# A two-layer hybrid backbone on one core: the splits of queries and keys keep the place in which they are traced

## The chip, the cores and the metric

The kernel runs on 1 core of one Trainium2 chip. The metric is the time of one execution on the device in microseconds (us); the median of 3 runs is given, and one execution was profiled. The engines are named as the profile names them: PE (TensorE, with PEld for its weight loads), DVE (VectorE), ACT (ScalarE), POOL (GpSimd), SP (the engine that issues most DMAs).

## The reference, cut to what matters

The model has two layers over 512 latent tokens and 256 context tokens of width 1024. Each layer is a half-step SwiGLU FFN, four parallel groups of heads over one input projection, an output projection, and a second half-step FFN. The change touches two of the four groups, both attention:

```
for l in range(DEPTH):                        # 2
    need_ctx = l < DEPTH - 1                  # the last layer gives no context output
    ...
    ya = s5_mixer(...)                        # a state-space scan
    yb = natten_mixer(q, k, v, rpb)           # neighbourhood attention, 4 heads of 64, bias table
    yc = gqa_mixer(q, k, v, gq, gk)           # 4 query heads, 2 key heads, qk-RMSNorm, rotary
    yd = rglru_mixer(...)                     # a gated recurrence
    h = h + gate * (concatenate([ya, yb, yc, yd]) @ w_out)

s = einsum('bqhgd,bkhd->bhgqk', q, k); p = softmax(s); o = einsum('bhgqk,bkhd->bqhgd', p, v)
```

Latent queries read context and latent keys (768 in all), context queries only context keys. In neighbourhood attention a latent query reads a window of 8 rows by 16 columns, plus the context. All of it is float32.

## The kernel before

**Precision by splitting.** PE multiplies in a float32 format of fewer bits (fp32r). A float32 operand x is therefore split into hi, its rounding to fp32r, and lo = x - hi. For the scores of attention the query tile holds hi of a head in 64 of its 128 partitions and lo in the other 64 (`stack_q`), and the key tiles hold kh (the hi part, once in each half) and kl (the lo part, once in each half). Two matmuls then give the score: one with kl as its moving operand (L796), one with kh (L797).

**The steps.** A split is an ACT instruction (the cast to hi: L963, L974, L984), then a DVE instruction that reads it (the subtraction: L964, L975, L985). Keys must then be copied to the other 64 partitions, which takes DMAs that POOL issues: in `stack_k` (gqa) one L977 for hi and one for lo, in `stack_ks` (neighbourhood attention, na) two L988 each for hi and lo, which fill the tiles of the second head from rows 64 to 128, and then one L989 each, which overwrites rows 64 to 128 of the first head's tile with its rows 0 to 64. So an L989 has to follow the two L988 that read what it overwrites. All of these copies are of 64 x 768 floats, 192 KB.

**The order of attention.** `attention()` (L817) goes through four groups: gqa(0), gqa(1), na(0), na(1). A group has 12 units in layer 0 (8 of latent queries and 4 of context queries) and 8 in layer 1. A unit has three stages: scores and softmax; transposes of the probabilities (L813, copied out by L815); the product with the values (L865). The stages of a unit stand 0, 2 and 3 units apart (LAGS), so that PE goes from one unit's scores to the transposes of another. The softmax is one DVE instruction (L805: add the bias or scale, take the maximum) and one of ACT (L806: exp). Each group has preparing steps, which are traced a few units ahead of its first unit: in gqa keys two units ahead and queries one, in na the bias 4, the keys 3, the queries 2 and the values 1 unit ahead. na also builds bias tiles on POOL (L1047 clears one, L1048 adds table and mask). In the last units of na(1) `part` splits finished rows for the output projection on POOL, L693 for hi and L696 for lo. Where an input projection is finished, `evac` takes it out of PSUM on DVE (L675, L679, L681).

**What sets the order.** The Tile framework traces the program and a scheduler (schedule_with_timeline_sim=True) orders each engine's instructions, by its own simulated timeline. `keep_in_program_order`, held as `self.pin`, makes an instruction keep its traced place among the pinned ones. In this kernel only PE's instructions in attention are pinned: scores (L796, L797), transposes (L813) and products with the values (L865). Each engine works through its order without skipping.

Of the kernel before, what the change touches and what calls it, by code (L numbers as in the profile page):

```python
# [10 lines left out]
F32 = mybir.dt.float32  # L11
F32R = mybir.dt.float32r
AF = mybir.ActivationFunctionType
ALU = mybir.AluOpType
# [6 lines left out]
TT = TL + TC  # L21
# [577 lines left out]
class Mixer:  # L599
# [357 lines left out]
    def stack_q(self, src, nt, scale=1.0, tag="g"):  # L957

        nc, out = self.nc, []
        for hh in range(2):  # L960
            a, b = 64 * hh, 64 - 64 * hh
            q = self.n.t(tag, F32R)
            nc.scalar.activation(q[a:a + 64, :nt], src[a:a + 64, :nt], AF.Copy, scale=scale)  # L963
            nc.vector.scalar_tensor_tensor(q[b:b + 64, :nt], src[a:a + 64, :nt], scale, q[a:a + 64, :nt].bitcast(F32),  # L964
                                           ALU.mult, ALU.subtract)
            out.append(q)
        return out

    def stack_k(self, src, hh, tag="g"):

        nc = self.nc
        a, b = 64 * hh, 64 - 64 * hh
        kh, kl = self.n.t(tag, F32R), self.n.t(tag, F32R)
        nc.scalar.copy(kh[a:a + 64, :TT], src[a:a + 64, :])  # L974
        nc.vector.tensor_sub(kl[a:a + 64, :TT], src[a:a + 64, :], kh[a:a + 64, :TT].bitcast(F32))  # L975
        for k in (kh, kl):
            nc.gpsimd.dma_start(k[b:b + 64, :TT], k[a:a + 64, :TT])  # L977
        return kh, kl

    def stack_ks(self, src):  # L980

        nc = self.nc
        kh, kl, kh2, kl2 = (self.n.t("g", F32R) for _ in range(4))
        nc.scalar.copy(kh[:, :TT], src)  # L984
        nc.vector.tensor_sub(kl[:, :TT], src, kh[:, :TT].bitcast(F32))  # L985
        for k, k2 in ((kh, kh2), (kl, kl2)):
            for a in (0, 64):
                nc.gpsimd.dma_start(k2[a:a + 64, :TT], k[64:128, :TT])  # L988
            nc.gpsimd.dma_start(k[64:128, :TT], k[0:64, :TT])  # L989
        return (kh, kl), (kh2, kl2)  # L990
# [679 lines left out]
```

## Time and profile before

| | us |
|---|---|
| median of 3 runs | 2868.43 (2867.08 to 2870.94) |
| profiled execution, time on the device | 2865.24 |
| its span | 2863.5 |
| busy in the span: PE | 2800.9 (98%) |
| DVE | 1730.1 (60%) |
| ACT | 909.4 (32%) |
| POOL | 759.4 (27%) |

The times of instructions below count from the start of the span. Attention lies at about 800 to 945 us in layer 0 and at 2305 to 2415 in layer 1; most of the rest is PE at work on the projections and the FFNs. In the rows a line number is that of the code, tiles are named without their running numbers, "x2" is two instructions in a row, and a bracket at the end of a row tells how long the engine sat idle before it and whose work ended that.

### The profile page before, as it was taken

The page shows a single profiled execution, that of the slowest core. Times are in us where ns is not written, and L with a number is a line of the kernel's source. Part 1 is how long each engine was busy: PE and PEld are TensorE (multiplying, and loading weights), DVE is VectorE, ACT ScalarE, POOL GpSimd, SP SyncE. Part 2 cuts the span into 40 slices and gives each one's busy share as a digit, 9 for nine tenths or more (in the row PEclk, how much of TensorE's full clock was granted, in tenths as well). Part 3 has the DMA queues.
Part 4 walks back from the last instruction along what each step waited for, and adds up shares of the span by engine and source line. Part 5 has one row for each costly group of instructions (what it writes and reads, how often), then busy time and mean ns, then how long its engine had stood idle before and what let it go on. Part 6 is the DMA issues. An engine that isn't in the chain of part 4 may idle for free.

```text
span 2863.5 us, 43435 instructions
## 1 busy us (share of the span) xinstructions
PE 2800.9 (98%) x17293; PEld 2429.0 (85%) x17293; DVE 1730.1 (60%) x3130; ACT 909.4 (32%) x1478; POOL 759.4 (27%) x957
## 2 busy tenths in 40 slices
PE   7999999999999999999999999999999999999998
PEld 4888888888877888888888888888888888899998
DVE  6868477676857566464634775465565876444445
ACT  3212122235546422212213321222224655322223
POOL 2822243222323311000001266423412434201001
PEclk8999999999999999999999999999999999999999
DMA  6445334354324333232212335233254444222231
GB/s 226 137 109 168 111 98 136 112 183 137 105 62 86 104 100 114 76 109 96 97 51 68 116 102 138 89 120 97 81 160 142 120 119 101 77 94 83 89 96 53
DMA packets 295900, 312.12 MB, mean 109 GB/s; under 512 B 58991, under 2 KB 243202, under 8 KB 295698
## 3 DMA queue, kind: packets, MB, share of 16 engines
q1 hardware_dynamic: 266990, 293.97, 32.2%
q0 software_dynamic: 5664, 12.59, 1.9%
q10 hardware_dynamic: 23044, 2.78, 0.7%
q8 instruction: 137, 2.24, 0.3%
q14 instruction: 65, 0.53, 0.1%
HBM read 276.09 MB, written 29.02 MB: 107 GB/s over the span
## 4 chain that ended last, share of the span: by engine, by line
PE 72%; DVE 5%; issue 1%; DMA 1%; ACT 1%; POOL 1%; SPq 0%; DVEq 0%; ACTq 0%; POOLq 0%
PE pi L390 41%; PE po L390 20%; PE po L1239 4%; PE po L865 1%; DVE acc L256 1%; PE pt L813 1%; PE ps L796 1%; PE pl L737 1%; DMA wa<-in_w_ada_dram 1%; DVE wl L380 1%; PE ps L797 0%; PE pa L263 0%; DMA W<-s5w 0%; PE px L1146 0%; DMA wr<-in_w_ffn_out_dram 0%
## 5 line engine op out<-in xcount | busy, mean ns | idle before, releaser
L390 PE MATMUL pi<-g,wh 128*128 128x258 f32 (+2 forms) x6656 | 1408.1, 330 | 8.2 <-DVE l L681 3.1
L390 PEld LDWEIGHTS pi<-g,wh 128*128 128x128 f32 x6656 | 1100.3, 191 | 131.8 <-issue 14.6
L390 PE MATMUL pi<-g,wl 128*128 128x258 f32 (+2 forms) x3328 | 825.3, 328 | 0.7 <-DVE wl L380 0.7
L379 ACT CAST wh<-wr 128x1024 fp32r<-128x1024 f32 (+3 forms) x380 | 339.0, 892 | 1405.2 <-PE pi L390 669.7
L390 PEld LDWEIGHTS pi<-g,wl 128*128 128x128 f32 x3328 | 607.0, 191 | 59.4 <-DVE wl L380 1.5
L390 PE MATMUL po<-l,wh 128*128 128x512 f32 (+1 forms) x2464 | 566.3, 344 | 1.2 <-DVE e L496 0.8
L390 PEld LDWEIGHTS po<-l,wh 128*128 128x128 f32 x2464 | 387.8, 188 | 64.3 <-issue 3.8
L460 POOL TENSOR_TENSOR l<-z,l 128x768 fp32r<-128x768 f32 (+1 forms) x88 | 159.0, 1806 | 1065.0 <-ACT l L459 958.9
L380 DVE TENSOR_TENSOR wl<-wr,wh 128x1024 fp32r<-128x1024 f32 (+3 forms) x380 | 404.3, 1064 | 54.3 <-ACT wh L379 51.5
L256 DVE SCALAR_TENSOR_TENSOR acc<-wa,s,acc 128x512 f32<-128x512 f32 x448 | 358.3, 849 | 40.8 <-DMA wa<-in_w_ada_dram 40.0
L496 DVE SCALAR_TENSOR_TENSOR e<-po,gt,e 128x512 f32<-128x512 f32 (+1 forms) x296 | 176.2, 631 | 305.2 <-PE po L390 251.2
L390 PE MATMUL po<-l,wl 128*128 128x512 f32 (+1 forms) x1232 | 337.1, 343 | 1.0 <-DVE wl L380 0.9
L454 DVE TENSOR_TENSOR z<-pi,R 128x768 f32<-128x768 f32 (+2 forms) x91 | 78.4, 865 | 301.3 <-PE pi L390 301.3
L390 PEld LDWEIGHTS po<-l,wl 128*128 128x128 f32 x1232 | 194.5, 188 | 32.9 <-DVE wl L380 2.4
L449 DVE COPY bc<-pi 128x2 f32<-128x2 f32 x88 | 13.8, 157 | 187.7 <-PE pi L390 187.7
L459 ACT CAST l<-z 128x768 fp32r<-128x768 f32 (+1 forms) x88 | 69.0, 784 | 160.9 <-DVE z L456 160.9
L1548 POOL TENSOR_TENSOR ww<-AR,BB 128x256 f32<-128x256 f32 x32 | 25.1, 786 | 338.2 <-PE pw L1567 306.8
L456 DVE SCALAR_TENSOR_TENSOR z<-z,pi,z 128x512 f32<-128x512 f32 (+1 forms) x154 | 107.8, 735 | 5.5 <-ACT z L452 0.8
L317 POOL TENSOR_TENSOR ssq<-ssq,sq 128x768 f32<-128x768 f32 (+1 forms) x35 | 67.8, 1936 | 161.6 <-ACT sq L316 161.6
L452 ACT ACTIVATE z<-z,bc 128x512 f32<-128x512 f32 (+1 forms) x154 | 90.3, 627 | 61.0 <-DVE z L450 49.9
L450 DVE TENSOR_TENSOR z<-pi,R 128x768 f32<-128x768 f32 (+1 forms) x88 | 77.5, 881 | 3.7 <-ACT R L367 3.7
L1239 PE MATMUL po<-l,wh 128*128 128x512 f32 (+1 forms) x264 | 72.0, 356 | 0.0
(349 smaller groups left out, 2597.9 us busy)
## 6 DMA issues: line engine op xcount, KB each, us to landing
wr<-in_w_ffn_in_dram SPq DMA_DIRECT2D x88, 1024.0 KB
wa<-in_w_ada_dram SPq DMA_DIRECT2D x64, 1024.0 KB
wr<-in_w_ffn_out_dram SPq DMA_DIRECT2D x48, 512.0 KB
wr<-in_w_ffn_out_dram SPq DMA_DIRECT2D x32, 640.0 KB
wr<-in_w_in_dram SPq DMA_DIRECT2D x16, 1024.0 KB
W<-s5w SPq DMA_DIRECT2D x32, 256.0 KB
wr<-in_w_out_dram SPq DMA_DIRECT2D x8, 1024.0 KB
l<-in_w_ada_dram SPq DMA_DIRECT2D x24, 256.0 KB
```

What stands on the lines that cost most here:

```text
L256: nc.vector.scalar_tensor_tensor(acc[r], raw[:, k], s, acc[r], ALU.mult, ALU.add)
L379: nc.scalar.copy(hi[:, :kn], raw[:, :, o:o + P])
L380: nc.vector.tensor_sub(lo[:, :kn], raw[:, :, o:o + P], hi[:, :kn].bitcast(F32))
L390: nc.tensor.matmul(dst, lhsT=wt[:, k, :], rhs=xt[:, a:b], start=(k == 0 and i == 0), stop=(k == kn - 1 and i == 2))
L450: nc.vector.tensor_mul(ta[:, :nt], pa[:, 256:256 + nt], self.R[:, :nt])
L452: nc.scalar.activation(ta[:, a:b], ta[:, a:b], AF.Silu, bias=bc[:, i:i + 1])
L454: nc.vector.tensor_mul(tb[:, a:b], p, self.R[:, a:b])
L456: nc.vector.scalar_tensor_tensor(tb[:, a:b], tb[:, a:b], pb[:, 254 + i:255 + i], ta[:, a:b], ALU.add, ALU.mult)
L459: nc.scalar.copy(uh[:, :nt], tb[:, :nt])
L460: nc.gpsimd.tensor_sub(ul[:, :nt], tb[:, :nt], uh[:, :nt].bitcast(F32))
L496: self.nc.vector.scalar_tensor_tensor(self.h[j][:, a:b], ps[:, a:b], gate[:, j, i:i + 1], self.h[j][:, a:b], ALU.mult, ALU.add)
L1239: self.nc.tensor.matmul(dst, lhsT=wt[:, k, :], rhs=xt[:, a:b], start=(c == 0 and i == 0), stop=(c == NT - 1 and i == 2))
```

## The change

The ACT and the DVE instruction of each split are given to `self.pin`: six instructions in three functions. Nothing else is edited.

```diff
@@ stack_q
-            nc.scalar.activation(q[a:a + 64, :nt], src[a:a + 64, :nt], AF.Copy, scale=scale)
-            nc.vector.scalar_tensor_tensor(q[b:b + 64, :nt], src[a:a + 64, :nt], scale, q[a:a + 64, :nt].bitcast(F32),
-                                           ALU.mult, ALU.subtract)
+            self.pin(nc.scalar.activation(q[a:a + 64, :nt], src[a:a + 64, :nt], AF.Copy, scale=scale))
+            self.pin(nc.vector.scalar_tensor_tensor(q[b:b + 64, :nt], src[a:a + 64, :nt], scale, q[a:a + 64, :nt].bitcast(F32),
+                                                    ALU.mult, ALU.subtract))
@@ stack_k
-        nc.scalar.copy(kh[a:a + 64, :TT], src[a:a + 64, :])
-        nc.vector.tensor_sub(kl[a:a + 64, :TT], src[a:a + 64, :], kh[a:a + 64, :TT].bitcast(F32))
+        self.pin(nc.scalar.copy(kh[a:a + 64, :TT], src[a:a + 64, :]))
+        self.pin(nc.vector.tensor_sub(kl[a:a + 64, :TT], src[a:a + 64, :], kh[a:a + 64, :TT].bitcast(F32)))
@@ stack_ks
-        nc.scalar.copy(kh[:, :TT], src)
-        nc.vector.tensor_sub(kl[:, :TT], src, kh[:, :TT].bitcast(F32))
+        self.pin(nc.scalar.copy(kh[:, :TT], src))
+        self.pin(nc.vector.tensor_sub(kl[:, :TT], src, kh[:, :TT].bitcast(F32)))
```

The built programs show what moves. A row gives the line, the operation, the tile written and the tiles read with their running numbers, and the shape; - is a row that stood here before, + one that stands here now.

VectorE in layer 0, in the first half of gqa(0). L975 of g_7993 is the lo of gqa(1)'s keys, the L964 of g_8033 and g_8036 of its queries, L985 of g_8304 and g_8637 the lo of the keys of na(0) and na(1), the L964 of g_8329 and g_8332 the queries of na(0):

```order
 L380 TENSOR_TENSOR wl_9081<-wr_9078,wh_9080 128x1024
-L975 TENSOR_TENSOR g_7993<-e_6807,g_7992 64x768
-L964 SCALAR_TENSOR_TENSOR g_8033<-e_6682,g_8033 64x768
-L964 SCALAR_TENSOR_TENSOR g_8036<-e_6682,g_8036 64x768
-L985 TENSOR_TENSOR g_8304<-l_7567,g_8303 128x768
-L964 SCALAR_TENSOR_TENSOR g_8329<-l_7407,g_8329 64x768
-L964 SCALAR_TENSOR_TENSOR g_8332<-l_7407,g_8332 64x768
-L985 TENSOR_TENSOR g_8637<-l_7665,g_8636 128x768
 L675 COPY bc_7971<-pi_7922 128x2
```

All seven leave this place and stand further down in the order, spread over the units of gqa(0), gqa(1) and na(0); the evacuation (L675) now follows the weight split (L380) at once.

POOL in layer 0, in the last units of na(0), ahead of na(1). g_8636 and g_8637 are kh and kl of the first head of na(1), g_8638 and g_8639 those of the second; e_8739 and e_8740 are bias tiles of na(1), l_8934 and l_8952 hi parts for the output projection:

```order
+L988 DMA g_8638<-g_8636 64x768 x2
+L988 DMA g_8639<-g_8637 64x768 x2
 L1047 MEMSET e_8739 128x256
 L1048 TENSOR_TENSOR e_8739<-e_8596,e_8257 128x256
 L1047 MEMSET e_8740 128x256
+L989 DMA g_8636<-g_8636 64x768
 L1048 TENSOR_TENSOR e_8740<-e_8605,e_8257 128x256
 L693 TENSOR_SCALAR l_8934<-z_7427 128x768
 L693 TENSOR_SCALAR l_8952<-z_7430 128x768
+L989 DMA g_8637<-g_8637 64x768
```

The six copies for na(1) stood before na(0)'s bias tiles, right behind those for na(0); now they stand in the last units of na(0), and that of kl comes behind two L693.

POOL in layer 1, at the same place. g_21858 and g_21859 are kh and kl of the first head of na(1), g_21860 and g_21861 those of the second. Before:

```order
L977 DMA g_21301<-g_21301 64x768
L988 DMA g_21587<-g_21585 64x768 x2
L988 DMA g_21588<-g_21586 64x768 x2
L988 DMA g_21860<-g_21858 64x768 x2
L989 DMA g_21585<-g_21585 64x768
L988 DMA g_21861<-g_21859 64x768 x2
L989 DMA g_21586<-g_21586 64x768
L989 DMA g_21858<-g_21858 64x768
L989 DMA g_21859<-g_21859 64x768
```

With the change:

```order
L988 DMA g_21860<-g_21858 64x768 x2
L988 DMA g_21861<-g_21859 64x768 x2
L1047 MEMSET e_21892 128x256
L1048 TENSOR_TENSOR e_21892<-e_21535,e_21533 128x256
L1047 MEMSET e_21893 128x256
L1048 TENSOR_TENSOR e_21893<-e_21544,e_21533 128x256
L1047 MEMSET e_21956 128x256
L1048 TENSOR_TENSOR e_21956<-e_21816,e_21533 128x256
L989 DMA g_21858<-g_21858 64x768
L1047 MEMSET e_21957 128x256
L989 DMA g_21859<-g_21859 64x768
```

The copies for na(1) have gone from behind the L977 of gqa(1) to the bias tiles of na(0)'s last units, with three pairs of L1047 and L1048 between the L988s and the first L989.

## Rows read from the trace of the kernel before

**Rows 1.** The page, parts 1 and 4: busy time, and the chain by engine.
```profile
PE 2800.9 (98%) x17293; PEld 2429.0 (85%) x17293; DVE 1730.1 (60%) x3130; ACT 909.4 (32%) x1478; POOL 759.4 (27%) x957
...
PE 72%; DVE 5%; issue 1%; DMA 1%; ACT 1%; POOL 1%; SPq 0%; DVEq 0%; ACTq 0%; POOLq 0%
```

**Rows 2.** Waits of PE, 800 to 1000 us: total us, times, longest.
```profile
PE ps L796 <- DVE l L681: 4.1, 3, 2.5
...
PE py L1175 <- POOL z L1163: 1.5, 1, 1.5
```

**Rows 3.** Waits of PE, 2300 to 2450 us.
```profile
PE ps L796 <- DVE l L681: 0.3, 1, 0.3
```

**Rows 4.** Windows: us, busy of PE, PEld, DVE, ACT, POOL, granted clock, DMA share, GB/s.
```profile
827.00:831.00 4.00, 4.00 (x17) 3.58 (x18) 0.56 (x1) 1.90 (x5) 0.00 (x0) 0.57 0.00 0
872.00:885.00 13.00, 10.07 (x78) 8.09 (x77) 11.97 (x21) 9.75 (x18) 4.88 (x10) 0.87 1.06 245
905.00:908.00 3.00, 2.60 (x19) 2.28 (x20) 2.29 (x5) 1.05 (x3) 1.12 (x2) 1.00 0.00 0
924.00:930.00 6.00, 5.51 (x54) 4.51 (x55) 4.73 (x14) 3.85 (x12) 5.96 (x6) 1.00 0.02 4
2404.00:2412.00 8.00, 7.68 (x87) 6.84 (x86) 6.50 (x17) 4.80 (x12) 4.79 (x9) 1.00 0.00 0
```

**Rows 5.** Timeline of DVE, layer 0: start us, us, instruction.
```profile
803.05 3.65 DVE L964 SCALAR_TENSOR_TENSOR e<-e,e 64x768 fp32r<-64x768 f32 x2
...
868.00 1.94 DVE L964 SCALAR_TENSOR_TENSOR g<-e,g 64x768 fp32r<-64x768 f32 x2
...
872.93 0.96 DVE L985 TENSOR_TENSOR g<-l,g 128x768 fp32r<-128x768 f32 x1
```

**Rows 6.** Timeline of PE, layer 0, first score after the burst, first of gqa(1).
```profile
875.34 0.77 PE L796 MATMUL ps<-e,e 128*128 128x512 f32 x1 [2.48 <-DVE l L681]
...
881.45 0.48 PE L796 MATMUL ps<-g,g 128*128 128x512 f32 x1
```

**Rows 7.** Views by line: issue of L988 (ns), landing of L977, landing of L989.
```profile
L988 POOL DMA_DIRECT2D g<-g x16: 512/519/519, 868.8 to 2354.9; - x16
...
DMA to landing us min/median/max: 2.5/2.6/5.0
...
DMA to landing us min/median/max: 4.5/6.6/10.8
```

**Rows 8.** Timeline, layer 0, ahead of na(0): DVE, and PE's first score of na(0).
```profile
901.26 1.02 DVE L805 CUSTOM_DVE_ANT_0 P<-ps,zero,rq 128x768 f32<-128x768 f32 x1 [1.44 <-PE ps L797]
...
907.61 0.36 PE L796 MATMUL ps<-g,g 128*128 128x256 f32 x1
```

**Rows 9.** Timeline, layer 0, ahead of na(1); the last is its first score.
```profile
922.57 0.73 ACT L806 ACTIVATE P<-P,mx 128x512 f32<-128x512 f32 x1 [0.24 <-DVE mx L805]
...
923.68 0.69 DVE L805 CUSTOM_DVE_ANT_0 P<-ps,e 128x512 f32<-128x512 f32 x1 [0.72 <-PE ps L797]
...
925.00 0.31 POOL L1047 MEMSET e<- 128x256 f32 x1
...
926.09 4.24 POOL L693 TENSOR_SCALAR l<-z 128x768 fp32r<-128x768 f32 x2
...
928.55 0.36 PE L796 MATMUL ps<-g,g 128*128 128x256 f32 x1
```

**Rows 10.** Timeline, layer 1, ahead of na(0): DVE, and PE's first score of na(0).
```profile
2383.08 1.02 DVE L805 CUSTOM_DVE_ANT_0 P<-ps,zero,rq 128x768 f32<-128x768 f32 x1 [1.60 <-PE ps L797]
...
2389.43 0.36 PE L796 MATMUL ps<-g,g 128*128 128x256 f32 x1
```

**Rows 11.** Timeline, layer 1, ahead of na(1); the last is its first score.
```profile
2400.12 0.73 ACT L806 ACTIVATE P<-P,mx 128x512 f32<-128x512 f32 x1 [0.40 <-DVE mx L805]
...
2401.03 0.69 DVE L805 CUSTOM_DVE_ANT_0 P<-ps,e 128x512 f32<-128x512 f32 x1 [0.40 <-PE ps L797]
...
2405.71 0.37 PE L796 MATMUL ps<-g,g 128*128 128x256 f32 x1
```

## The prediction

> **What bounds the kernel now.** I read the page first: TensorE (PE) is busy for 98% of the span, and the chain that ended last is PE for 72%, VectorE (DVE) 5%, every other engine 1% or less [rows 1]. So the time moves only where PE comes to wait, or stops waiting. The touched steps lie in two stretches, the attention of layer 0 (about 800 to 945 us) and of layer 1 (2305 to 2415). Next come PE's waits there. In layer 0 the largest sum is 4.1 us for scores held up by an evacuation on DVE (L681), the longest 2.5; 1.5 us more goes to a table step of POOL (GpSimd) [rows 2]. In layer 1 the same evacuation costs 0.3 [rows 3]. That is all that the change can win; what it can lose has no such ceiling. Waits of 1.5 us and more can also lower the clock: in 827 to 831, behind a wait, the granted clock is 0.57, that is half speed (1.2 of 2.4 GHz) for most of it; in 872 to 885, around the 2.5 us wait, it is 0.87, in the NA stretches 1.00 [rows 4]. The first row prices such a slump: 4.00 us x (1 - 0.57) = 1.7.
>
> **What the change moves.** No instruction is added or dropped, and PE's order in attention stays as it was; the splits move. Before, the splits of gqa(1), na(0) and na(1) were one burst per layer. In layer 0 it holds DVE from the L964 pair at 868.00 to the last L985, which ends at 873.9 [rows 5]; the evacuation for which PE waits until 875.34 comes behind it [rows 6]. The POOL copies followed at once, well before na(0) and na(1) need them (first scores at 907.61 and 928.55 [rows 8, 9]). After, each split stands where it is traced, one to four units ahead of its group, and its copies behind it, among POOL's bias tiles (L1047, L1048) and, in layer 0, the out-projection splits (L693). A key split is a chain: ACT cast (L984), DVE subtract (L985), four L988 on POOL, then two L989, which overwrite rows that the L988s read. The group's first score multiplies the lo half first (L796), so it waits for the last L989.
>
> **Prices.** L985 takes 0.96 [rows 5]; the cast beside it I put at the same, 0.9. Issuing a copy takes POOL 0.52. From issue to landing it is 2.5 at best and 2.6 in the median on L977, but 4.5 to 10.8 on L989 [rows 7]. Bounds of a landing: 2.5 and 6.6, the L989 median. I take 2.5, because the L989 rows of before are from the burst, where the DMA engines were full (1.06 in 872 to 885), and they are empty where the copies go now: 0.00, 0.02 and 0.00 [rows 4]. On POOL a memset (L1047) takes 0.3 and a pair of L1047 and L1048 1.1 (from 925.00 to the L693 at 926.09 [rows 9]), so an L1048 0.8.
>
> The Trainium skill, "DMA: Bandwidth & Descriptors", section "Anatomy of one DMA", gives about 2.0 us plus bytes over 436e3 for a copy issued by GpSimd, an estimated 2.45 us for 192 KB, whatever the load. The L989 rows of before do not agree with that, those of L977 do; with the rule the sum below stays as it is, with the L989 median it would be 16 us more.
>
> **Place by place, layer 0.** *gqa(0):* its L964 pair, 3.65 us at 803.05 [rows 5], leaves the stretch in which PE waits 1.5 for POOL [rows 2]; the splits come later, before scores that they can still meet. -0.4, between -1.5 and +1. *gqa(1):* with the burst gone the evacuation ends some 2 us earlier and the wait of 2.48 shrinks to about 0.5. But the keys' L975 now stands behind the softmax and the copy of the unit whose score ended that wait: 873.3 for the score, 1.4 for it, 1.0 for the softmax, its copy and L975 give 877 to 878.2, and with 2.5 for the landing the keys are there at up to 880.7, where the first score ran at 881.45 before [rows 6]. So -0.7, between -2.5 and +1.5. *na(0):* L985 comes behind the softmax that ends at 902.3 [rows 8], so lo is ready at 903.25, the last L988 issued at 904.3, two pairs later it is 906.5, the last L989 starts at 907.0 and lands at 909.5; the first score ran at 907.61. +1.9, between 0 (if something hides it) and 6.0.
>
> *na(1)* is the large term [rows 9]. ACT's exp ends at 923.4 with its read, the cast at 924.3. The L988s of hi go out from 924.3 to 925.3. DVE's softmax ends at 924.4, L985 at 925.35, the L988s of lo are out at 926.4. Then POOL's own order: a pair and one memset to 927.8, L989 of hi to 928.3, one L1048 to 929.1, **two L693 of 2.12 each (4.24) to 933.4**, and only then L989 of lo, landing at 935.9. The first score ran at 928.55: PE waits 7.4 more. Everything on PE is behind that score, since its order is fixed; DVE and ACT run dry, too. Behind such a wait I count one slump of the clock, 1.7 less a tenth, since PE is busy for 5.51 of 6 us there anyway [rows 4]: 1.5. Together +8.9. Without the L693s ahead it would be 7.4 - 4.2 = 3.2; with the L989 median 11.5 and 1.5. Bounds 3 and 13.
>
> **Layer 1.** *gqa(0)* and *gqa(1):* POOL and DVE have room; the 0.3 of [rows 3] may go. -0.3, between -1 and +1. *na(0):* L985 fits into DVE's idle 1.60 before 2383.08 [rows 10], lo is ready at 2382.9, the L988s are out at 2384.0; four memsets (1.2) and two L1048 (1.6) follow, the last L989 starts at 2387.3 and lands at 2389.8, against a first score at 2389.43. +0.4, between 0 and 4.5. *na(1)* [rows 11]: exp to 2400.95, cast to 2401.85, L988s of hi to 2402.85; L985 ends at 2402.7, L988s of lo are out at 2403.9; three pairs (3.3) to 2407.2, L989 of hi to 2407.7, a memset, L989 of lo from 2408.0, landing at 2410.5. First score before: 2405.71. +4.8, and 1.5 for the clock: +6.3, between 3 and 10.4.
>
> Some short waits of before go inside the new long ones: -0.7 (estimate: under a tenth of the new waits). **Sum:** -0.4 - 0.7 + 1.9 + 8.9 - 0.3 + 0.4 + 6.3 - 0.7 = +15.4. The profiled execution took 2865.24, so 2880.6; the median of the runs is 3.2 above it, 2868.43, which gives 2883.8, **2884**.
>
> What carries this is that POOL does its queue in order: the copy of lo can't pass the L693s. The Trainium skill, "PSUM — Partial Sum Buffer", section "Engine vs sequencer instructions", says the same of the queues of ScalarE, VectorE and GpSimd: strictly first in, first out. It speaks against this change, which puts copies behind other work; if it did not hold for copies, na(1) of layer 0 would cost the 3.2 above and the time would be 2879.6.
>
> **Rivals.** *The waits are mostly covered.* If the lo copies are not what the first scores wait for, only the splits' own time counts: three more steps of 0.96 on DVE ahead of PE's copies, of which PE sees about 1.7 at na(0), 2.4 at na(1) and 1.5 in layer 1's na(1). With -0.4, -0.7, -0.3 and -0.7 that is +3.5: 2872. For it: DVE is busy for only 4.73 of 6 us there [rows 4]. Against: the first score reads the tile that L989 writes. 0.15.
> *Faster: only the burst counts.* The 2.5 and 1.5 of [rows 2], the 0.3 of [rows 3] and the slump of 872 to 885 (13 x 0.13 = 1.7) go: -6.0, 2862.4. It needs all four NA copies in time; the deciding point is L989 of lo issued by 926.0 at na(1) of layer 0, and in POOL's order the L693s stand ahead of it. 0.08.
> *The copies land slowly.* If L989 takes its 4.5 of before even on empty engines, four places get 2.0 each: +8, 2892; with 6.6, 2900. For it: no L989 of before was faster. 0.15.
> *That the change does nothing* is out: the built order shows the splits moved. The forecast keeps 0.60, 0.02 is left for the unforeseen.
>
> **Numbers.** 0.2% (5.7 us) is what a measurement can tell from no change: 2862.7 to 2874.2. Faster 0.08; same 0.16, the covered case and a little; slower 0.76. The range 2870 to 2893 takes in the covered case, the slow copies at 4.5 and the bounds of the two large terms one at a time; outside lie the faster case and copies at 6.6.
>
> **What would show it.** Right: PE's list of waits has scores (L796) held by DMA of g, of about 7, 5 and 2 us, the longest behind a POOL L693 pair; granted clock below 1 behind the first two; the 2.5 us wait at 875 shrunk; landings of L988 and L989 near 2.5. Wrong: those scores released by DVE or ACT instead; L989 issued before the L693s end; waits at na(1) under 3 us; or a new wait at gqa(1), where the keys come late, of over 2 us.

## The result, and the profile after

| | before | after |
|---|---|---|
| median of 4 runs, us | 2867.76 (2864.69 to 2870.94) | 2896.06 (2895.71 to 2899.38) |
| profiled execution, us | 2865.24 | 2896.15 |
| its span, us | 2863.5 | 2894.4 |

The changed kernel is slower: ratio 1.0102, 95% interval 1.0089 to 1.0114, that is 28.3 us. The direction was forecast, the size was not: 2884 was predicted, with 2893 as the upper end of the range.

Parts 1 and 4 of the page of after (busy time; the chain by engine), to be held against [rows 1]:

```profile
PE 2809.1 (97%) x17293; PEld 2436.5 (84%) x17293; DVE 1741.7 (60%) x3130; ACT 906.1 (31%) x1478; POOL 754.8 (26%) x957
...
PE 71%; DVE 5%; DMA 2%; issue 1%; ACT 1%; POOL 1%; SPq 0%; DVEq 0%; POOLq 0%; ACTq 0%
```

PE executes the same 17293 matmuls and is busy 8.2 us longer; some 7 of them are the same matmuls of na(0) and na(1) in both layers at the lower clock. The rest of the 31 us of the span is waiting. In the chain the DMA share went from 1% to 2%, and nothing else grew. PE's waits (total us, times, longest) from 800 to 1000 us say the same; the last row is from 2300 to 2460:

```profile
PE ps L796 <- DMA g<-g: 12.1, 2, 6.4
PE pt L813 <- DVE l L815: 3.7, 2, 3.6
PE ps L796 <- DMA e<-e: 2.6, 1, 2.6
...
PE ps L796 <- DVE l L681: 1.4, 2, 0.7
...
PE ps L796 <- DMA g<-g: 5.0, 1, 5.0
```

The evacuation wait of [rows 2] fell from 4.1 to 1.4, as meant. In its place scores wait for copied keys (DMA of g), 12.1 us in two waits in layer 0 and 5.0 in one in layer 1. Two more waits stood in no forecast: a transpose waits 3.6 for DVE, and the first score of gqa(0) waits 2.6 for its own keys (DMA of e).

**Stage by stage.** PE's order of scores, transposes and products in attention is the same in all versions but e4, so a stage can be cut by the starts of the same two matmuls in both traces. The table gives how much longer than before each stage took, in us, from one profiled execution each. gqa(0) is the stretch from 795 to 821 us of before, which ends ahead of that group's first score. "Between" are the stretches ahead of na(0) and of na(1) of layer 0 that neither group's column holds. In e4 nine transposes of each na group's values stand 4 units earlier in PE's order, so that of its cells for between, na(0) and na(1) only the sum, +6.3, can be compared.

| | gqa(0) | gqa(1) | between | na(0) | na(1) | L1 na(0) | L1 na(1) | ratio of runs, 95% |
|---|---|---|---|---|---|---|---|---|
| forecast | -0.4 | -0.7 | - | +1.9 | +8.9 | +0.4 | +6.3 | |
| after | -1.23 | +4.57 | 0 | +6.04 | +11.47 | +1.60 | +7.18 | 1.0102 (1.0089 to 1.0114) |
| after, another run | -1.23 | +4.87 | 0 | +5.71 | +11.43 | +2.86 | +7.30 | |
| before, another run | +0.04 | +1.40 | 0 | 0 | 0 | 0 | 0 | |
| e1 | 0 | -3.15 | 0 | +5.72 | +10.61 | +1.81 | +6.76 | 1.0086 (1.0066 to 1.0107) |
| e2 | 0 | +0.50 | 0 | +5.63 | +2.95 | +0.69 | +1.07 | 1.0058 (1.0038 to 1.0078) |
| e3 | -1.23 | +5.06 | 0 | +2.88 | +10.67 | +1.01 | +7.24 | 1.0104 (1.0084 to 1.0124) |
| e4 | -1.23 | -3.17 | +6.4 | -0.87 | +0.75 | +0.25 | -0.47 | 1.0027 (1.0015 to 1.0039) |
| e5 | -1.21 | +4.57 | 0 | +2.74 | +5.95 | +5.30 | +6.97 | 1.0095 (1.0075 to 1.0115) |
| e6 | -1.23 | -3.16 | 0 | +4.75 | +10.50 | +2.84 | +9.20 | 1.0089 (1.0067 to 1.0111) |
| e7 | -1.21 | 0 | 0 | 0 | 0 | 0 | 0 | 1.0000 (0.9992 to 1.0008) |
| e8 | -1.21 | -3.17 | +0.6 | +4.56 | 0 | 0 | 0 | 1.0004 (0.9996 to 1.0013) |
| e9 | -1.25 | -3.16 | +2.6 | +1.21 | -0.55 | 0 | 0 | 1.0005 (0.9996 to 1.0014) |

The third and fourth line price the table itself. Two runs of one program agree within 0.4 us at the na places of layer 0 and at na(1) of layer 1, within 1.4 at gqa(1) and at na(0) of layer 1. Elsewhere, above all from 2276 to 2342 us, a stage of one and the same program moves by 1 to 2 us from one profile to the next. One such stretch is that behind gqa(0)'s column, 821 to 838 us: the second run of before needs 1.5 us less there than the first. PE waits 1.8 us for ACT in both, but the granted clock from 827 to 831 is 0.57 in the first (the row by which the prediction prices a slump) and 1.00 in the second. So a wait of that length can leave the clock where it was.

The six places of after sum to +29.6 of the 30.9 us that its profiled execution lost. So the loss is in attention; the question is what makes each place.

The -1.2 of gqa(0) is no gain yet. It is PE's wait of 1.5 us for POOL's table step, which falls to 0.3 wherever gqa(0)'s splits are pinned. In the stretch behind it, which no column holds, the first score then waits 2.3 to 3.0 us for the copied keys. Over both stretches, 795 to 838 us, after takes 1.4 us less than the first run of before and 0.1 more than the second.

### The profile page after: what moved, and what is told of

It is laid out like the page before. It is cut to its first block, busy times and chain, and to the rows that moved or that the text cites. A ratio compares the mean times of both kernels' runs of the same rounds, so it can differ in the third digit from the quotient of the medians.

```text
span 2894.4 us, 43416 instructions
## 1 busy us (share of the span) xinstructions
PE 2809.1 (97%) x17293; PEld 2436.5 (84%) x17293; DVE 1741.7 (60%) x3130; ACT 906.1 (31%) x1478; POOL 754.8 (26%) x957
## 4 chain that ended last, share of the span: by engine, by line
PE 71%; DVE 5%; DMA 2%; issue 1%; ACT 1%; POOL 1%; SPq 0%; DVEq 0%; POOLq 0%; ACTq 0%
PE pi L390 41%; PE po L390 19%; PE po L1239 4%; PE po L865 1%; PE pt L813 1%; DVE acc L256 1%; PE ps L796 1%; DMA g<-g 1%; DVE wl L380 1%; PE pl L737 1%; PE ps L797 0%; PE pa L263 0%; DMA wa<-in_w_ada_dram 0%; DVE P L805 0%; PE px L1146 0%
## 5 line engine op out<-in xcount | busy, mean ns | idle before, releaser
L380 DVE TENSOR_TENSOR wl<-wr,wh 128x1024 fp32r<-128x1024 f32 (+3 forms) x380 | 409.3, 1077 | 52.9 <-ACT wh L379 50.2
```

Of the source, the lines that this page charges most:

```text
L380: nc.vector.tensor_sub(lo[:, :kn], raw[:, :, o:o + P], hi[:, :kn].bitcast(F32))
```

## The experiments

Most expectations set two theories against each other, in their own words: the keys' copies come too late for the score that needs them (through POOL's queue, or by when they are traced), or the splits' own time on DVE and ACT, or the engine that issues the copies, makes the loss. All ratios are to before on the same chip.

### e1: only the na keys pinned

The four `self.pin` of `stack_q` and `stack_k` are taken back:

```diff
-            self.pin(nc.scalar.activation(q[a:a + 64, :nt], ...
+            nc.scalar.activation(q[a:a + 64, :nt], ...
...
-        self.pin(nc.scalar.copy(kh[a:a + 64, :TT], src[a:a + 64, :]))
+        nc.scalar.copy(kh[a:a + 64, :TT], src[a:a + 64, :])
```

> Only the key splits of neighbourhood attention (L984, L985) are pinned; those of gqa and all query splits are left to the scheduler. Theory A (three separate causes: the copy of gqa(1)'s kl lands in 6.3 us because weight loads fill the DMA engines then; at na(0) the two L964 take 5.28 us beside POOL's bias tiles; at na(1) the L989 of kl stands behind two L693): against before, PE loses nothing at gqa(0), gains 1 to 2 us at gqa(1) since most of the burst ahead of the evacuation is gone and the gqa(1) keys stay in it, loses about 6 at na(0), 11 at na(1), and 1.5 and 7 in layer 1: about 24 us more than before. Rival B (the splits themselves are late, whichever they are, and the copies' place does not matter): about a third of the 28 us of the change, under 12 us more than before.

Measured: 2889.48 against 2864.23, 1.0086, +25 us. The two pinned instructions of `stack_ks` alone make na(0), na(1) and layer 1's na(1) what they are in after, within 1 us. That is the +24 of theory A. The queries of na(0), though not pinned, moved too: their two L964 take 4.10 us beside POOL's bias tiles. gqa(1) gains 3.15 instead of losing 4.6: its keys, unpinned, are split in time, so its loss does not come from na's pins.

### e2: only the queries pinned

```diff
-        self.pin(nc.scalar.copy(kh[:, :TT], src))
-        self.pin(nc.vector.tensor_sub(kl[:, :TT], src, kh[:, :TT].bitcast(F32)))
+        nc.scalar.copy(kh[:, :TT], src)
+        nc.vector.tensor_sub(kl[:, :TT], src, kh[:, :TT].bitcast(F32))
```

(and the same two in `stack_k`.)

> Only the query splits (L963, L964) are pinned; the copies of the keys then stand well ahead of na(1) in the order of layer 0, and ahead of the bias tiles of na(0). Theory A: no long DMA wait at na(1) of layer 0, so that place costs only what the L964s cost beside POOL (0 to 3 us); at na(0) the L964 pair is stretched to 3 to 5 us if POOL builds bias tiles beside it, and PE loses 3 to 6 us there; gqa(1) within 1.5 us of before: in all 4 to 10 us more than before. Rival B (late splits as such): na(1) still loses 5 or more; in all over 12.

Measured: 1.0058, +17 us, more than expected. na(0) again loses 5.6, with other instructions in other places. DVE ahead of na(0), and POOL beside it (start, us, instruction):

```profile
904.44 1.94 DVE L964 SCALAR_TENSOR_TENSOR g<-l,g 64x768 fp32r<-64x768 f32 x2
...
906.41 2.92 DVE L985 TENSOR_TENSOR g<-l,g 128x768 fp32r<-128x768 f32 x1
```

```profile
906.59 0.87 POOL L1048 TENSOR_TENSOR e<-e,e 128x256 f32<-128x256 f32 x1
...
907.65 0.86 POOL L1048 TENSOR_TENSOR e<-e,e 128x256 f32<-128x256 f32 x1
```

While POOL issues DMAs the two L964 take 1.94; the L985 behind them, 0.96 in [rows 5], takes 2.92 beside two L1048. The copies of lo can leave only after it. So two things came together that the expectation had apart: the scheduler also moved key splits that were not pinned, and a split beside POOL's table steps takes three times as long.

### e3: the L988 of both tiles first, POOL's steps pinned too

If the copy of lo waits behind POOL's other work, an order in which it doesn't should free the scores.

```diff
                 nc.gpsimd.dma_start(k2[a:a + 64, :TT], k[64:128, :TT])
-            nc.gpsimd.dma_start(k[64:128, :TT], k[0:64, :TT])
+                self.pin(nc.gpsimd.dma_start(k2[a:a + 64, :TT], k[64:128, :TT]))
+        [self.pin(nc.gpsimd.dma_start(k[64:128, :TT], k[0:64, :TT])) for k in (kh, kl)]
...
-            G.memset(bt[hh][:, 256:512], 0.0)
+            self.pin(G.memset(bt[hh][:, 256:512], 0.0))
```

(the L988 are pinned as well, and the `tensor_add` of L1048.)

> The change, with the copies L988 and L989 (all four L988 ahead of the two L989) and the bias tiles (L1047, L1048) pinned too, so that the copies stand ahead of the bias tiles traced behind them and ahead of the L693s. Theory A: at na(1) of layer 0 the L989 of kl starts some 6 us earlier and PE's wait for it falls from 6.4 us to 0 to 3; in layer 1's na(1) from 5.0 to about 2.9; at na(0) the L964 pair runs beside DMA issues instead of bias tiles and takes under 3 us instead of 5.3, the wait of 3.6 us for L815 goes; gqa(1) keeps its wait of 5.6. In all 10 to 18 us more than before, that is 10 to 18 less than the change. Rival B: as slow as the change within 5 us. If the issue of DMAs on POOL is what stretches the L964s, the pair still takes 4 us or more.

Measured: 1.0104, +30 us, where less was expected. Both mechanisms acted, and the time stayed. At na(0) the same two L964 as in after now meet a POOL that issues DMAs, and take 1.94 (after: 5.28); the place costs 2.88 instead of 6.04. At na(1) the score waits 1.36 for its keys instead of 6.44, yet the place costs 10.67. DVE (the first row is na(0)) and PE:

```profile
908.87 1.94 DVE L964 SCALAR_TENSOR_TENSOR g<-l,g 64x768 fp32r<-64x768 f32 x2
...
939.32 0.69 DVE L805 CUSTOM_DVE_ANT_0 P<-ps,e 128x512 f32<-128x512 f32 x1 [3.05 <-POOL e L1048]
```

```profile
940.30 0.55 PE L796 MATMUL ps<-g,g 128*128 128x256 f32 x1 [1.36 <-DMA g<-g]
...
945.32 1.97 PE L865 MATMUL po<-PT,l 128*64 128x128 f32 x14 [2.35 <-ACT PT L815]
```

The bias tile (e, from POOL's L1048) is late now, the softmax on DVE waits 3.05 for it, and PE gets a wait of 2.35 a few us on. POOL itself stands still for 2.43 and 1.00 us ahead of the two L989 (at 936.15 and 937.66), until the L988 have landed, with the bias tiles behind them. Around na(1) POOL has copies, bias tiles and L693 to do one after the other, and here the one that came last held PE up. [rows 4] had shown how full POOL is there: busy for 5.96 of 6 us from 924 to 930.

### e4: all preparing steps 4 units earlier

```diff
-                at.setdefault(max(len(todo) - len(prep) + i, 0), []).append(f)
+                at.setdefault(max(len(todo) - len(prep) - 4 + i, 0), []).append(f)
```

> The change, with every group's preparing steps traced four units further ahead (keys of gqa(1) six units ahead instead of two, of na seven instead of three). Theory A: the copies have landed before the first scores at all four places; no wait of PE for DMA of g over 1 us, and the time is between 4 us faster and 6 us slower than before. Rival B (splits among the units cost PE by themselves, through DVE and ACT): 8 to 20 us slower than before, with waits for L815 and L806 in place of those for DMA.

Measured: 2871.04 against 2864.23, 1.0027 (1.0015 to 1.0039), +6.8 us, just above the 6 at most that were expected: three quarters of the loss are gone. gqa(1) gains 3.17, and layer 1's na(1) costs nothing. In PE's list no score waits for a DMA of g any more. What is left in the trace lies between the groups of layer 0 (the sum of +6.3, in short waits of up to 1.0 us, most of them for the copies of L815, and a granted clock of 0.55 from 918 to 924), in a wait of 2.5 us for a copy of L815 in gqa(1) of layer 1, behind an L985 that takes 2.04 beside POOL's arithmetic, and in one new wait for keys of gqa(0) in layer 1:

```profile
PE ps L796 <- DMA e<-e: 3.4, 1, 3.4
```

Why that copy is later there than in after (0.3) was not followed up.

### e5: SP issues the na copies instead of POOL

```diff
-                nc.gpsimd.dma_start(k2[a:a + 64, :TT], k[64:128, :TT])
-            nc.gpsimd.dma_start(k[64:128, :TT], k[0:64, :TT])
+                nc.sync.dma_start(k2[a:a + 64, :TT].bitcast(F32), k[64:128, :TT].bitcast(F32))
+            nc.sync.dma_start(k[64:128, :TT].bitcast(F32), k[0:64, :TT].bitcast(F32))
```

> The change, with the neighbourhood copies L988 and L989 issued by SP instead of POOL; the order of everything else on POOL, DVE, ACT and PE stays. Theory A (at both na(1) the scores wait because POOL's queue holds the copies behind its own work): PE's wait for DMA of g at na(1) of layer 0 falls from 6.4 us to 0 to 2.5, at na(1) of layer 1 from 5.0 to 0 to 2; the loss at na(1) falls from 11.5 to 3 to 6 us and from 7.2 to 1 to 3; gqa(1) of layer 0 stays at +4.6 and na(0) at +4 to +6, since the L964s are stretched by bias tiles as before. In all 12 to 19 us more than before. Rival (the splits come too late for any queue, the copies land late wherever they are issued): the waits at na(1) stay over 4 us and the total within 4 us of the change.

Measured: 1.0095, +27 us, where about half was expected. In layer 0 the copies no longer stand behind the L693, and na(1) costs 5.95 instead of 11.47; na(0) falls to 2.74, with its two L964 at 1.94 beside an idle POOL. But layer 1's na(0) rises to 5.30. In layer 1 it costs 6.97, hardly less than the 7.18 with POOL. The whole chain there, ACT, SP's queue and PE:

```profile
2420.94 0.82 ACT L984 CAST g<-l 128x768 fp32r<-128x768 f32 x1
```

```profile
2421.78 2.68 SPq L988 DMA_DIRECT2D g<-g  x4
...
2426.79 1.29 SPq L989 DMA_DIRECT2D g<-g  x2
```

```profile
2430.37 0.55 PE L796 MATMUL ps<-g,g 128*128 128x256 f32 x1 [4.34 <-DMA g<-g]
```

The L988 go out at once behind the cast, until 2424.46. The L989, which overwrite what the L988 read, start when these have landed, 2.3 us later, and their own landing, 2.3 us after 2428.08, starts the score. From the end of the cast to the score that is 8.6 us with nothing else in the way, of which PE waits 4.34. Four of the 8.6 are SP's issuing. So here it is not POOL's order alone: keys traced 3 units ahead are too late for either queue, since two landings stand one behind the other. In after the same shows on POOL: the four L988 of this place land 4.0 to 4.2 us after their issue, the last at 2430.1, and the L989 of lo goes out at 2430.7, so without the bias tiles between them it could hardly have gone sooner.

### e6: the keys of gqa(1) 4 units earlier

```diff
-        for prep, units in [self.gqa(0), self.gqa(1), self.na(0), self.na(1)]:
+        for g, (prep, units) in enumerate([self.gqa(0), self.gqa(1), self.na(0), self.na(1)]):
...
-                at.setdefault(max(len(todo) - len(prep) + i, 0), []).append(f)
+                at.setdefault(max(len(todo) - len(prep) - (4 if g == 1 else 0) + i, 0), []).append(f)
```

> The change, with only gqa(1)'s keys and queries traced four units further ahead; all else in place. Theory A (the copy of gqa(1)'s kl was issued when weight loads fill the DMA engines): in layer 0 gqa(1) turns from +4.6 us to about -3 against before, and na(0) and na(1) stay at +6 and +11.5: 20 to 22 us more than before. Rival (the loss at gqa(1) is DVE and ACT work among the units): gqa(1) stays over +2.

Measured: 1.0089, +25 us, a little over the 20 to 22 expected; gqa(1) went from +4.57 to -3.16, and the rest stayed within 2 us of after. The copy of lo goes out some 10 us earlier than in after (874.82):

```profile
863.77 0.54 POOL L977 DMA_DIRECT2D g<-g  x1 [0.61 <-DVE g L975]
```

It lands in 2.6 us, and no score of gqa(1) waits for it. The whole of that place's loss is the time at which its keys and queries are split.

### e7: only gqa(0) pinned

```diff
+        pin = self.pin if tag == "e" else (lambda i: i)
...
-            self.pin(nc.scalar.activation(q[a:a + 64, :nt], ...
+            pin(nc.scalar.activation(q[a:a + 64, :nt], ...
```

> Only gqa(0)'s splits are pinned; gqa(1), na(0) and na(1) are left to the scheduler and stay one burst. Theory A: the 1.2 to 1.6 us that the change gained at gqa(0) of layer 0 stay, nothing else moves: 0 to 3 us faster than before. Rival: the gain is given back in layer 1, where the scheduler's order shifts too: within 2 us either way.

(and the same in `stack_k`.) Measured: 1.0000 (0.9992 to 1.0008) over 12 runs. gqa(0) shows its -1.21 and every other column 0, but the stretch from 821 to 838 us takes 2.0 us more than in the first run of before, with one new wait: the first score waits 2.9 us for a DMA of e. So pinning gqa(0) moves a wait from POOL's table step to the keys, and its trace shows no gain either.

### e8 and e9: layer 0 alone, with places chosen by hand

Layer 1 keeps the order of before. In layer 0 each preparing step gets its own distance from its group's first unit (order of the numbers: as the steps are traced; in na bias, keys, queries, values). e8 has

```diff
+AT = ((-2, -1), (-6, -5), (-4, -10, -8, -1), (-4, -18, -15, -1))
...
-            for i, f in enumerate(prep):
-                at.setdefault(max(len(todo) - len(prep) + i, 0), []).append(f)
+            for i, f in zip(AT[g] if self.l == 0 else range(-len(prep), 0), prep):
+                at.setdefault(max(len(todo) + i, 0), []).append(f)
```

and e9 the same with (-4, -10, -9, -1) as the last.

> Layer 0 alone is pinned, and each split has a unit of its own in the middle of the group before: gqa(1) keys 6 and queries 5 units ahead, na(0) keys 10 and queries 8, na(1) keys 18 and queries 15; values and bias stay where they were; layer 1 is as before. Theory A: gqa(0) -1.3, gqa(1) -3, na(0) and na(1) between 0 and +2 each, since the copies have landed and POOL builds no bias tiles beside the splits: 1 to 4 us faster than before. Rival B (any split among the units costs PE 1 to 2 us): 2 to 8 us slower.

> As the spread version before it (layer 0 alone pinned, gqa(1) keys 6 and queries 5 units ahead, na(0) keys 10 and queries 8), but na(1)'s keys 10 and queries 9 units ahead of it, which is inside na(0), away from the burst of bias tiles that POOL built beside na(1)'s query split there (one L964 took 3.36 us instead of 0.95). Theory A (a DVE instruction that reads and writes SBUF makes no progress while POOL computes): each L964 and L985 of na takes under 1.1 us unless a bias tile runs beside it, na(0) falls from +4.6 to under +1.5, gqa(0) and gqa(1) keep -1.2 and -3.2, na(1) 0 to +1.5: 2 to 5 us faster than before. Rival (the 3 us were lost for another reason, DVE has no room there): na(0) still +3 or more, within 1 us of before.

Measured: e8 1.0004 (0.9996 to 1.0013), e9 1.0005 (0.9996 to 1.0014); a gain of 1 to 5 us was expected of each. e8 is the cleanest view of why. Its keys are there in time, na(1) costs nothing, and the place of na(0) still loses 4.56, 3.1 of it a wait of PE for a copy (L815) behind the second of these two L964, which split na(1)'s queries. DVE, and POOL beside it:

```profile
896.57 0.95 DVE L964 SCALAR_TENSOR_TENSOR g<-l,g 64x768 fp32r<-64x768 f32 x1
...
898.61 3.36 DVE L964 SCALAR_TENSOR_TENSOR g<-l,g 64x768 fp32r<-64x768 f32 x1
```

```profile
898.18 0.86 POOL L1048 TENSOR_TENSOR e<-e,e 128x256 f32<-128x256 f32 x1
...
899.24 0.85 POOL L1048 TENSOR_TENSOR e<-e,e 128x256 f32<-128x256 f32 x1
...
900.29 0.84 POOL L1048 TENSOR_TENSOR e<-e,e 128x256 f32<-128x256 f32 x1
```

Two instructions of one form, 2 us apart: 0.95 while POOL waits for a landing and issues a copy, 3.36 while it computes bias tiles. e9 moves that: one of its two L964 takes 2.05 beside the end of one L1048 and the whole of the next, the other 0.95, and na(0) costs 1.21, as its theory A had it. But 2.6 us more go between the groups, where na(1)'s splits now stand. From 795 to 957 us its stages sum to 1.1 us less than before, the only gain of the whole layer that an arrangement kept, and less than the 1.4 by which two runs of before differ at gqa(1) alone. From 2276 to 2342 us its trace lies 3.9 us above that of the first run of before and 2.3 above that of the second, in a part whose order is that of before but for a few instructions; no run ties this to the edit. No version here beats before by more than its measurement can tell.

### The same programs once more

> The kernel before, profiled a second time, to see how far single stages differ from one profile to the next with the same instructions. Theory A: the stages of attention in layer 0 (795 to 957 us) and the four na places of layer 1 repeat within 0.3 us, so the losses named there are the change's; the stage before attention of layer 1 (2276 to 2342 us), where all kernels differ by 1 to 4 us, differs here too, by 1 us or more, and is not the change's. Rival: 2276 to 2342 repeats within 0.3 us, and the 0.8 to 3 us there belong to the kernels.

> The change, profiled a second time. Theory A: against the kernel before again +4.6 us at gqa(1), +6.0 at na(0), +11.5 at na(1) of layer 0, +1.6 and +7.2 at na(0) and na(1) of layer 1, each within 0.5 us; the stages between and ahead of them differ by up to 2 us. Rival: one of the five places differs by over 1.5 us from the first profile, and its size is chance.

Measured: 2864.42 and 2899.81, one run each, beside 2865.76 for before. Their stages are the two repeats in the table above. Of before, the na places repeat within 0.1 us, but gqa(1) differs by 1.4 and the stretch from 821 to 838 by 1.5, more than the 0.3 expected; 2276 to 2342 differs by 1.7, as expected. Of after, four of the five places repeat within 0.5 us; layer 1's na(0) differs by 1.3, short of the rival's 1.5. In both runs the loss is where the table has it.

## Why the prediction was wrong, point by point

**What was right.** The direction, and for two of its large terms the mechanism. At na(1) of layer 0 the copy of lo stands behind the L693 pair and the score waits for it, 6.44 us where 7.4 was worked out. POOL and PE of after (a bracket: idle before, and what ended it):

```profile
938.30 4.25 POOL L693 TENSOR_SCALAR l<-z 128x768 fp32r<-128x768 f32 x2
942.49 0.58 POOL L989 DMA_DIRECT2D g<-g  x1
```

```profile
945.11 0.58 PE L796 MATMUL ps<-g,g 128*128 128x256 f32 x1 [6.44 <-DMA g<-g]
```

From the issue to the score are 2.6 us, and the landings of L989 in after are 2.5, 2.6 and 3.0 (least, median, most), not the 4.5 to 10.8 of [rows 7]. So the landing of 2.5 was right for na, and the rival of slow copies was wrong there. In layer 1, na(1) was put at +6.3 and came to +7.18. The number is partly luck: e5 adds that POOL's order was only part of its cause, since the chain itself is too long there, and the landing of the L988 (4.0 to 4.2), for which an L989 has to wait, stood in no term.

**The first failed step: the landing at gqa(1)** (-0.7 forecast, +4.57 measured). The prediction had the L975 end at 877 to 878.2 and added 2.5 for the landing. After:

```profile
869.97 0.47 PE L796 MATMUL ps<-e,e 128*128 128x512 f32 x1 [0.72 <-DVE l L681]
...
881.16 0.77 PE L796 MATMUL ps<-g,g 128*128 128x512 f32 x1 [5.64 <-DMA g<-g]
```

```profile
873.33 0.95 DVE L975 TENSOR_TENSOR g<-e,g 64x768 fp32r<-64x768 f32 x1
```

```profile
874.82 0.54 POOL L977 DMA_DIRECT2D g<-g  x1 [2.52 <-PE ps L796]
```

The wait behind the burst shrank from 2.48 to 0.72, as forecast. The split ended at 874.28; the trace of after runs 3.6 us ahead of that of before here, so in the prediction's times this is 877.9, also as forecast. But from the issue at 874.82 to the score are 6.3 us. The stretch (us, busy of PE, PEld, DVE, ACT, POOL, granted clock, DMA share, GB/s):

```profile
872.00:876.00 4.00, 2.36 (x22) 1.71 (x18) 3.74 (x8) 3.98 (x8) 0.84 (x2) 1.00 0.80 167
876.00:881.00 5.00, 0.00 (x0) 0.00 (x0) 2.62 (x4) 1.56 (x4) 0.00 (x0) 0.99 1.04 268
```

PE does nothing for 5 us, and the DMA engines are full; of their time from 870 to 885 us 53.7% of all 16 goes to SP's queue of loads (a weight tile of 1 MB among them) and 10.0% to the copies. From 875.5 to 877.9 SP's queue moves 713 packets and POOL's a single one; the 80 packets of the copy of lo run from 878 to 880.1. The landings of L977, 2.6 in the median before [rows 7], are now 6.2:

```profile
DMA to landing us min/median/max: 2.5/6.2/6.8
```

The prediction had this in its hands. It set the slow L989 of before down to full DMA engines, read 1.06 for 872 to 885 in [rows 4], and then wrote "they are empty where the copies go now" of all copies. That is true of the three na stretches it checked and false of gqa(1), which lies in the very window of the 1.06. A landing of 6.3 in the same sum gives 883.3 to 884.5 where the score ran at 881.45 before, a wait of 2 to 3 us, which the prediction itself had named as a sign of being wrong. (The score of after ran at 884.8 in those times.)

The same step failed at gqa(0), where the number hides it. "Before scores that they can still meet" was the forecast for its splits; but its copies, which landed in 2.6 and 2.7 us at 807 to 808 before, go out at 813.6 and 814.7 now, beside loads again (DMA share 1.04 from 815 to 818), land in 6.8 and 6.5, and the first score waits 2.6 us for them.

No run changes the load alone, so that it is the cause is read from the traces. What DVE does beside the copy does not tell the cases apart: it was busy for 4.94 of 5 us from 905 to 910 in after, where the two L989 landed in 2.5 and 3.0. The Trainium skill, "DMA: Bandwidth & Descriptors", section "Anatomy of one DMA", gives an estimated 2.45 us for such a copy. The landings of 2.5 agree, those of 6.2 to 6.8 do not; that fit has no term for what else the DMA engines carry, and that it holds "whatever the load" was the prediction's reading. Here the measurement decides.

**The second failed step: na(0)** (+1.9 forecast, +6.04 measured). The forecast followed the chain of the keys alone; the split of the queries behind it, two casts on ACT (L963) and two L964 on DVE, stood in no term. The copies came in good time, issued at 907.77, and PE waited for something else:

```profile
907.71 0.55 PE L813 MATMUL pt<-ident,l 128*128 128x128 f32 x3 [1.58 <-ACT e L886]
...
911.81 0.90 PE L813 MATMUL pt<-ident,l 128*128 128x128 f32 x3 [3.56 <-DVE l L815]
```

ACT was held by the two casts, which stand ahead of the copy (L886, at 907.30) that ends the first wait:

```profile
904.63 1.71 ACT L963 ACTIVATE g<-l 64x768 fp32r<-64x768 f32 x2
```

DVE was held by the two L964, beside POOL's bias tiles:

```profile
905.55 5.28 DVE L964 SCALAR_TENSOR_TENSOR g<-l,g 64x768 fp32r<-64x768 f32 x2
```

```profile
905.93 0.87 POOL L1048 TENSOR_TENSOR e<-e,e 128x256 f32<-128x256 f32 x1
...
909.15 0.86 POOL L1048 TENSOR_TENSOR e<-e,e 128x256 f32<-128x256 f32 x1
```

Against before, PE is idle 4.7 us longer at this place (the waits of 1.58 and 3.56, less what it waited there before) and busy 1.3 longer with the same matmuls (granted clock 0.50 from 910 to 914): together the 6.04. That POOL stretches the L964 is shown: in e3, with the same DVE order, the pair takes 1.94, in e8 the two cases stand side by side, and e2 does the same to an L985. But that is only half of the price. In e3 and e5, where the pair takes 1.94, the place still costs 2.88 and 2.74, with the same wait of 1.58 for L886: this half is the query split standing there at all. That the casts on ACT cause that wait is read from their place ahead of L886; no run moved them alone. The row that would have told it was quoted ahead of the prediction. [rows 5] has the L964 pair twice, 3.65 at 803.05 and 1.94 at 868.00, and the prediction used both numbers without asking why they differ. POOL of before at the first:

```profile
803.31 2.58 POOL L769 TENSOR_TENSOR z<-l,e 128x768 f32<-128x768 f32 x1
```

The Trainium skill, "SBUF — State Buffer", section "SBUF: two separate sides", states the rule: VectorE and GpSimd share a pair of ports, an exclusive lock, and a VectorE instruction with two inputs in SBUF contends with a GpSimd instruction that reads SBUF. The trace agrees, with 0.95 against 3.36 in e8. The prediction looked at POOL's queue as what delays copies, and not as what slows the splits.

**The third: the price behind the long wait** (na(1), +8.9 forecast, +11.47 measured). The long wait was 1 us shorter than forecast and the loss 2.6 larger. The windows:

```profile
937.00:943.00 6.00, 1.48 (x6) 0.78 (x5) 4.48 (x10) 1.59 (x4) 5.99 (x5) 0.50 0.16 33
943.00:946.00 3.00, 0.89 (x4) 0.89 (x5) 0.00 (x0) 0.00 (x0) 2.90 (x3) 0.50 0.34 66
946.00:949.00 3.00, 3.00 (x22) 2.36 (x21) 1.39 (x3) 0.82 (x2) 3.00 (x6) 0.50 0.00 0
```

The granted clock is 0.50, the lower of the two levels (1.2 GHz), for 12 us. PE is busy for 5.37 of them (1.48 + 0.89 + 3.00), and half of that, 2.7, is lost to the clock. It falls ahead of the long wait, behind three short ones (0.72, 0.36, 0.63) that the forecast did not have; from 931 to 937 it is already 0.87. Over the whole place PE is busy 3.8 us longer than before with the same matmuls, where one slump of 1.5 was assumed: this is the term that was mis-sized. With another wait of 0.80 later and one of 0.19 the waits are 9.1, against 1.5 in before; 7.7 + 3.8 are the 11.47.

**Layer 1's na(0)** came to +1.60 and, in the other run, +2.86, where +0.4 (0 to 4.5) was forecast: inside its bounds, and too unsteady to say more.

**The sum.** gqa(1) was 5.3 us off, na(0) 4.1, na(1) 2.6, layer 1's na(0) 1.2 and na(1) 0.9, gqa(0) -0.8, together 13.2 in the profiled execution; the forecast of 2880.6 for it missed by 15.5, and the rest lies outside the six places and in the 0.7 taken off for waits that merge. Five of the six errors go the same way: landings, splits and clock were priced by their best rows or left out. The range took the bounds of the two large terms one at a time. Those two stayed inside them; it was gqa(1), at +4.57 against a bound of +1.5, na(0), at its bound of 6.0, and na(1) together that passed the upper end.

**What stays open.** What DMA load alone does to a copy's landing, which no run varied; how much of e4's 6.8 us is its new wait in layer 1, and why that copy is late; and the stretch from 2276 to 2342, which differs by 1 to 4 us between versions with almost the same order there.

## What to carry to other kernels

A duration holds for the neighbours it was measured beside: before it goes into a sum, look at what the DMA engines and POOL do at the place to which the instruction moves, and where two rows of one form differ, find out why first. Spreading a burst pays only if each piece still ends well ahead of its consumer; here the burst cost PE one wait of 2.48 us, and splits that start just ahead of their group cost 28 us. Part of that is the chain itself: cast, subtract and two landings in a row took 8.6 us in e5, four of them issuing. When several jobs share one in-order engine that has no time left (POOL at na(1)), a better order among them moved the wait (e3) and didn't remove it; taking the copies off that engine (e5) halved the loss of that place. When times of two traces are compared, take off first by how much one runs ahead of the other there.

## What the runs showed of the hardware

- DVE steps with two inputs in SBUF take 2 to 3.5 times as long beside POOL arithmetic: L964 0.95 alone, 2.05 beside the end of one L1048 and the whole of the next (e9), 3.36 across three (e8); L985 0.96 and 2.92 (e2). Beside POOL issuing DMAs they keep their 0.95 (e3: 1.94 for two).
- In e8 the L964 that began at 898.61 ended at 901.97, 0.84 us after the last of three L1048. Having 0.95 us of work of its own, it had made next to no headway beside all three in a row.
- A copy of 192 KB within SBUF lands in 2.5 us on idle DMA engines and in 6.2 to 6.8 beside a stream of loads (DMA share 0.80 to 1.04 at gqa(1)). Most of the difference lies ahead of its first packet: issued at 874.82, it moved its 80 packets from 878 to 880.1.
- Behind the same wait of 1.8 us PE's granted clock was 0.57 for 4 us in one run of before and 1.00 in another.
